# A two-layer encoder trunk: dense stages with a PSUM pool for each product bank, the last head's chunk in a tile of its own, and sums of squares on VectorE

## The chip, the cores and the metric

The kernel runs on one core of one Trainium2 chip. The metric is device time in microseconds for one execution; less is better. A core has engines that each work through a queue of their own in order: TensorE (PE in the profile; its weight loads are PEld), VectorE (DVE), ScalarE (ACT), GpSimd (POOL) and SyncE (SP), which issues DMA transfers. ScalarE issues some DMA transfers too. Matmul products land in PSUM, eight banks of 128 partitions by 512 f32 values; everything else lies in SBUF or in HBM.

## The reference

Two layers work on 1024 tokens of width 1024. In cut form:

```python
for i in range(2):
    h = rms_norm(x, norm_g[i])
    y = mixer_a(h, ...) if i == 0 else mixer_b(h, ...)   # attention, times silu(gate), @ w_out
    x = x + y
    g = sigmoid(rms_norm(x, ple_norm_g[i]) @ ple_w_gate[i])
    x = x + g * (p[i] @ ple_w_proj[i])
return rms_norm(x, final_norm_g)
```

`rms_norm(x, g)` is `x * rsqrt(mean(x*x) + 1e-6) * g`. Mixer A is 2-D neighbourhood attention of 16 heads with a bias table, mixer B grouped-query attention of 16 query and 4 key heads with normalised, rotated queries and keys. All is f32.

## The kernel before, in words

The program has four stages in a row: mixer A, dense stage 0, mixer B, dense stage 1. The mixers make the attention output times the gate, 128 channels (a pair of heads) at a time, and the dense stages do the rest of a layer: the output projection with the residual sum ("out"), and the gated input embedding ("ple").

**Numbers.** Each f32 operand of a projection is split into a high part, rounded to the matmul type f32r, and the low rest, and a product is three matmuls: high times high, high times low, low times high (`split3`, three calls of `mm`, L316). The activations stand transposed in two tiles, HTh and HTl, as [128 channels, 8 token tiles, 8 chunks of channels, 128 tokens]. `put` (L396 to L401) fills a chunk of four token tiles: ScalarE writes the high part (L400), VectorE the low one (L401). For the dense stages the chunks 0 to 6 of the mixer's output come back from HBM (`load_y`, L278, issued by ScalarE during the mixer's last head), and chunk 7, the last pair of heads, is written by `fin_last` (L471 to L480) straight from the mixer's end: VectorE multiplies (L472, L476; the second reads a PSUM bank "t" or "o" of the mixer for the second half of the tokens), ScalarE writes the high part (L479), VectorE the low one (L480).

**Weights** come in units of 128 x 1024 through two staging tiles (`Weights`, L184). `pump` is called once for each step of the program. It stages up to two units ahead (`stage`), but only `lag` (3) steps after the last split, and splits a unit no sooner than 3 steps after it was staged and when its pool has room: ScalarE copies the high part (L221), and VectorE makes the low part (L222) at the next step.

**A dense stage** (`dense_phase`, L1154) works in groups: "out" for token tiles 0 to 3, "out" for 4 to 7, then "ple" for the same; in dense stage 1 the last "ple" group is halved into tiles 4, 5 and tiles 6, 7. A group makes eight chunks of 128 output channels, each with the product over eight contraction steps, 24 matmuls, in two half-chunks (`parts`); the first group of a stage does the first halves of chunks 0 to 3 ahead of their second halves. Each chunk takes a PSUM bank from the pool `ps_d` (six banks, in turn); transposes use `ps_t` (two banks).

When a chunk's product is ready, `evac` reads it. For "out", VectorE adds it to the residual XR (L1224). For "ple", VectorE multiplies by the norm's factor (L1228), ScalarE applies tanh (L1229), and VectorE multiplies with the embedding and adds to XR (L1232, L1233). Then ScalarE squares the new chunk (L1216) and GpSimd adds the square to the group's sum `acc` (L1219); the first chunk's square starts the sum (L1213). These steps are put on short lists (`soon`, `rest`) that are worked off between half-chunks, one entry of `rest` at a step, so that each engine's queue is an order written out by hand. After a group come, as entries of `rest`, the eight `put`s for the next projection, the norm (`norm`: PE transposes `acc`, L1184, VectorE sums over tokens' rows, L1185, then L404 and GpSimd's power of -0.5, L405), and the spread of the factor over all partitions (`turn`: PE, L409, and a ScalarE copy, L1191). For the final groups the order is two empty entries, the norm, an empty one, the spread and the store (L1282, one multiplication for two chunks, the last on GpSimd).

The last group of all ends in `end` (L1248 to L1266): transposes of `acc` and of the last square, one reduction on VectorE (L1254), the factor, its spread, a ScalarE copy of the spread (L1261), and the multiplications with their stores (L1263 to L1266).

**Mixer B starts** with projections of keys and values: for each token tile, two items of 12 matmuls with 256 columns, whose products stand in turn in the one bank "d" and the bank "o", and are read by ScalarE (L996). What the last dense group left on `rest` is worked off between them.

**PSUM pools**, in the order of their banks: mixer A has "d" (0, 1), "s" (2, 3), "t" (4, 5), "o" (6, 7); a dense stage has `ps_d` (0 to 5) and `ps_t` (6, 7); mixer B has "d" (0), "s" (1 to 4), "t" (5, 6), "o" (7). A pool is opened where the stage before it closed its own. The framework puts in the waits that a tile needs before its memory is used again.

Of the kernel before, what the change touches and what calls it, by code (L numbers as in the profile page):

```python
# [11 lines left out]
F32 = mybir.dt.float32  # L12
F32R = mybir.dt.float32r
# [3 lines left out]
ALU = mybir.AluOpType  # L17
# [4 lines left out]
NT = 8  # L22
# [133 lines left out]
def trunk(ctx, tc, x, xT, wts, bias, gains, hgains, mask, rope, out):  # L156
# [13 lines left out]
    HTh = glob.tile([128, NT, KC, 128], F32R, name="HTh")  # L170
    HTl = glob.tile([128, NT, KC, 128], F32R, name="HTl")
# [106 lines left out]
    def load_y(l, t):  # L278
        for d, src in zip((HTh, HTl), yD[l]):
            act.dma_start(d[:, t, 0:7].bitcast(F32), src[t, :, 0:7])  # L280
# [73 lines left out]
    def proj_T(key, hf, alloc, evac, release=(), kstep=None):  # L354
# [3 lines left out]
        for k0, k1 in chunks(KC, kstep):  # L358
            def f(k0=k0, k1=k1):
# [3 lines left out]
                rh = HTh[:, 4 * hf:4 * hf + 4]  # L363
                rl = HTl[:, 4 * hf:4 * hf + 4]
                for k in range(k0, k1):
                    c = slice(k * 128, (k + 1) * 128)
                    split3(st["ps"], wh[:, c], wl[:, c], rh[:, :, k, :], rl[:, :, k, :], k == 0, k == KC - 1)
# [7 lines left out]
    def proj_N(keys, t, ncol, alloc, evac, release=(), kstep=None):  # L375
# [5 lines left out]
        for k0, k1 in chunks(nk, kstep):  # L381
            def f(k0=k0, k1=k1):
                if k0 == 0:
                    st["ps"] = alloc()
                for k in range(k0, k1):
                    wh, wl = WQ.get(keys[k // per])
                    c = slice((k % per) * ncol, (k % per + 1) * ncol)
                    split3(st["ps"], HTh[:, t, k, :], HTl[:, t, k, :], wh[:, c], wl[:, c], k == 0, k == nk - 1)
# [7 lines left out]
    def put(src, gi, hf, k, eng=None):  # L396
# [3 lines left out]
        act.activation(HTh[:, ts, k, :], src, AF.Copy, scale=g)  # L400
        dve.scalar_tensor_tensor(HTl[:, ts, k, :], src, g, HTh[:, ts, k, :], op0=ALU.mult, op1=ALU.subtract)  # L401
# [9 lines left out]
    def head_end(sb, h, hf, rs, Ops, ylive, layer, gg, talloc):  # L411
# [59 lines left out]
        def fin_last():  # L471
# [7 lines left out]
            act.activation(HTh[:, ts, 7, :], y3, AF.Copy)  # L479
            dve.tensor_tensor(HTl[:, ts, 7, :], y3, HTh[:, ts, 7, :], ALU.subtract)  # L480
# [53 lines left out]
    def mixer_a():  # L534
        with ExitStack() as es:
            one = es.enter_context(tc.tile_pool(name="aone", bufs=1))
            pd = es.enter_context(tc.tile_pool(name="apd", bufs=2, space=PSUM))
            psS = es.enter_context(tc.tile_pool(name="aps", bufs=2, space=PSUM))
# [29 lines left out]
            def v_first(hf, banks, k):  # L568
                wh, wl = WQ.get(("av", 0, k // 4))
                c = slice((k % 4) * 256, (k % 4 + 1) * 256)  # L570
                for i in range(3):
                    for t in range(4):
                        a = (HTh, HTh, HTl)[i][:, 4 * hf + t, k, :]
# [580 lines left out]
    def dense_phase(l):  # L1154
        with ExitStack() as es:
# [4 lines left out]
            ps_d = es.enter_context(tc.tile_pool(name="dps", bufs=6, space=PSUM))  # L1160
            ps_t = es.enter_context(tc.tile_pool(name="dpt", bufs=2, space=PSUM))
# [3 lines left out]
            WQ.cap[2] = WSLOTS  # L1165
            for c in range(4):
                WQ.get(("out", l, c))
# [3 lines left out]
            def alloc():  # L1171
                return ps_d.tile([128, 512], F32, name="d")
# [21 lines left out]
            def group(kind, ta, tb, final, to, gi):  # L1194
# [15 lines left out]
                def square(c):  # L1210
# [8 lines left out]
                    pool.tensor_tensor(acc, acc, sq, ALU.add)  # L1219
# [28 lines left out]
                def end(sq):  # L1248
                    ps = talloc()
# [132 lines left out]
```

## Time and profile before

| | us |
|---|---|
| three runs | 1554.23, 1554.27, 1555.39 (median 1554.27) |
| the profiled execution | 1555.67 |
| its span, first to last instruction | 1553.9 |
| PE busy | 1505.5 |
| VectorE busy | 996.4 |
| ScalarE busy | 857.6 |
| GpSimd busy | 401.7 |
| mean granted clock of TensorE | 0.991 |

Times in a row of a timeline are the start from the beginning of the span and the duration. In square brackets stands how long the engine had been idle before, and what ended the idle time as far as semaphores tell. "L316 PE MATMUL d<-HTh,wh" is a matmul issued on line 316 whose product goes to the tile "d" with HTh and wh as its operands; "x24" at a row's end are 24 merged instructions. Matmuls are pipelined, so the pace of a run of them is read from one start to the next and not from the duration. A busy share of PE over the whole span is an average over stages: what matters here is where PE has no work.

### The profile page before, as it was taken

Reading aid. Unit: us, or ns where it says so; the run is one execution under the profiler, and the core shown is the slowest. Engines: PE = TensorE matmul, PEld = TensorE weight load, DVE = VectorE, ACT = ScalarE, POOL = GpSimd, SP = SyncE. Lnnn points to the kernel's source line nnn. Section 1 sums busy time; section 2 is a strip of 40 time slices with the busy share of each in tenths; the row PEclk is TensorE's granted clock in tenths of the full one; section 3 lists DMA queues with packets and bytes.
Section 4 is the critical chain, followed back from the end, with each engine's and each line's share of the span. In section 5 each row is a group of like instructions: output and inputs, shape, how many; then the busy total and the mean of one; then the engine's idle time right before and its main releaser. Section 6 shows DMA issues by size and latency. Waiting matters only on the chain.

```text
span 1553.9 us, 24232 instructions
## 1 busy us (share of the span) xinstructions
PE 1505.5 (97%) x9058; PEld 1325.3 (85%) x9058; DVE 996.4 (64%) x1678; ACT 857.6 (55%) x1663; POOL 401.7 (26%) x507
## 2 busy tenths in 40 slices
PE   8999999999999899998999999999999999899997
PEld 8789889888988688888988889989888888778886
DVE  4675675576576334667867777677777887624475
ACT  7564554555456423335476666766667767513343
POOL 1231232223222032122512234445132200022133
PEclk9999999999999999999999999999999999999998
DMA  7221311221125942242200111111101214633122
GB/s 298 78 65 43 106 47 59 84 62 56 64 77 156 333 132 89 93 149 77 70 20 22 48 50 46 57 39 52 42 21 42 89 35 151 207 127 104 57 82 95
DMA packets 91621, 136.91 MB, mean 88 GB/s; under 512 B 13296, under 2 KB 54384, under 8 KB 91504
## 3 DMA queue, kind: packets, MB, share of 16 engines
q1 hardware_dynamic: 86496, 120.29, 23.8%
q10 hardware_dynamic: 5008, 15.08, 2.8%
q8 instruction: 71, 1.16, 0.3%
q14 instruction: 46, 0.38, 0.1%
HBM read 102.72 MB, written 32.62 MB: 87 GB/s over the span
## 4 chain that ended last, share of the span: by engine, by line
PE 74%; DVE 13%; ACT 8%; issue 3%; DMA 1%; ACTq 0%; POOL 0%; DVEq 0%; SPq 0%; POOLq 0%
PE d L316 47%; PE o L316 10%; PE s L316 8%; PE t L1074 5%; DVE PTl L1077 2%; PE t L663 2%; DVE mn L1058 2%; DVE wl L222 2%; DVE th L1232 1%; ACT PTh L1076 1%; DVE HTl L401 1%; DVE XR L1233 1%; ACT wh L221 1%; ACT HTh L400 1%; ACT P L1064 1%
## 5 line engine op out<-in xcount | busy, mean ns | idle before, releaser
L316 PE MATMUL d<-HTh,wh 128*128 128x512 f32 (+1 forms) x1080 | 419.0, 388 | 5.6 <-issue 4.7
L316 PE MATMUL d<-HTh,wl 128*128 128x512 f32 (+1 forms) x1080 | 409.7, 379 | 1.5 <-DVE wl L222 1.5
L316 PE MATMUL d<-HTl,wh 128*128 128x512 f32 (+1 forms) x1080 | 409.3, 379 | 0.0
L1077 DVE TENSOR_TENSOR PTl<-t,PTh 128x512 fp32r<-128x512 f32 x256 | 164.5, 684 | 123.8 <-ACT PTh L1076 123.0
L316 PEld LDWEIGHTS d<-HTh,wl 128*128 128x128 f32 x1080 | 203.9, 189 | 41.2 <-DVE wl L222 1.9
L316 PEld LDWEIGHTS d<-HTh,wh 128*128 128x128 f32 x1080 | 204.2, 189 | 37.1 <-issue 5.1
L316 PEld LDWEIGHTS d<-HTl,wh 128*128 128x128 f32 x1080 | 204.5, 189 | 30.2
L1064 ACT ACTIVATE P<-s,mn 128x1024 f32<-128x1024 f32 x128 | 142.6, 1114 | 58.6 <-DVE mn L1058 58.2
L1219 POOL TENSOR_TENSOR acc<-acc,sq 128x512 f32<-128x512 f32 (+1 forms) x62 | 75.6, 1219 | 368.5 <-ACT sq L1216 368.5
L1076 ACT ACTIVATE PTh<-t 128x512 fp32r<-128x512 f32 x256 | 139.5, 592 | 40.8 <-PE t L1074 40.1
L316 PE MATMUL d<-wh,HTh 128*128 128x256 f32 x544 | 153.9, 290 | 7.2 <-ACT sq L1216 4.3
L1058 DVE TENSOR_REDUCE mn<-s 128x1 f32<-128x1024 f32 x128 | 154.8, 1209 | 9.3 <-PE s L316 9.1
L316 PE MATMUL d<-wl,HTh 128*128 128x256 f32 x544 | 151.2, 285 | 0.0
L316 PE MATMUL d<-wh,HTl 128*128 128x256 f32 x544 | 151.1, 285 | 0.0
L1074 PE MATMUL t<-ident,P 128*128 128x128 f32 x1024 | 137.7, 275 | 8.2 <-DVE PTl L1077 5.9
L1074 PEld LDWEIGHTS t<-ident,P 128*128 128x128 f32 x1024 | 114.6, 141 | 24.5 <-DVE PTl L1077 18.5
L316 PE MATMUL s<-KA,QS 128*128 128x512 f32 (+2 forms) x384 | 133.7, 402 | 0.0
L316 PE MATMUL o<-PTh,V 128*128 128x256 f32 (+2 forms) x672 | 119.2, 288 | 3.2 <-ACT P L1064 1.1
L316 PE MATMUL s<-KB,QS 128*128 128x512 f32 (+2 forms) x384 | 121.6, 371 | 0.0
L222 DVE TENSOR_TENSOR wl<-wstage,wh 128x1024 fp32r<-128x1024 f32 x86 | 108.6, 1268 | 20.4 <-ACT wh L221 18.9
L316 PE MATMUL o<-PTl,V 128*128 128x256 f32 (+2 forms) x672 | 118.8, 288 | 0.3 <-DVE PTl L667 0.3
L1216 ACT ACTIVATE sq<-XR 128x512 f32<-128x512 f32 (+1 forms) x63 | 36.8, 585 | 142.9 <-DVE XR L1224 88.1
(178 smaller groups left out, 2623.4 us busy)
## 6 DMA issues: line engine op xcount, KB each, us to landing
wstage<-in_wts SPq DMA_DIRECT2D x92, 512.0 KB
rb<-rD SPq DMA_DIRECT2D x56, 128.0 KB
ppD<-th SPq DMA_DIRECT2D x24, 256.0 KB
pp<-ppD SPq DMA_DIRECT2D x24, 256.0 KB
XT<-in_xT SPq DMA_DIRECT2D x8, 512.0 KB
X<-in_x SPq DMA_DIRECT2D x8, 512.0 KB
XR<-in_xT SPq DMA_DIRECT2D x16, 256.0 KB
xD<-XR SPq DMA_DIRECT2D x16, 256.0 KB
```

Of the source, the lines that this page charges most:

```text
L221: act.activation(hi, s, AF.Copy)
L222: self.rest = lambda: dve.tensor_tensor(lo, s, hi, ALU.subtract)
L316: pe.matmul(ps, a, b, start=first, stop=last, skip_group_check=True)
L400: act.activation(HTh[:, ts, k, :], src, AF.Copy, scale=g)
L663: pe.transpose(ps[:, i], sp[:, i * 128:(i + 1) * 128], ident)
L1058: dve.tensor_reduce(mn, ps, axis=AX.X, op=ALU.min)
L1064: act.activation(p, ps, AF.Exp, bias=mn, scale=-1.0, accum_out=RS[h, hf][:, t:t + 1])
L1074: pe.transpose(ps[:, i], p[:, k * 128:(k + 1) * 128], ident)
L1076: act.activation(PTh[:, ks, c], ps, AF.Copy)
L1077: dve.tensor_tensor(PTl[:, ks, c], ps, PTh[:, ks, c], ALU.subtract)
L1216: act.activation(sq, xr, AF.Square)
L1219: pool.tensor_tensor(acc, acc, sq, ALU.add)
```

## The change

- The six banks of one pool `ps_d` become four pools of one bank each, taken in turn; the turn starts with bank 0 in dense stage 0 and with bank 1 in dense stage 1. `ps_t` gets four banks. In mixer A the pools "s" and "d" change places, so "s" has banks 0 and 1.
- Chunk 7 of HTh and of HTl goes into a tile of its own; `HTh(t, k)` and `HTl(t, k)` pick the tile.
- In the dense stages the weights' `lag` is 2 and not 3.
- The squares are added to `acc` by VectorE and not by GpSimd.
- In the final groups five empty entries instead of two stand ahead of the norm.
- At the end, matmuls with a column of 1/1024 make the mean of the squares in one product, in place of transposes and a reduction; the factor is spread into two banks, one for VectorE, one for ScalarE's copy; the stores are cut smaller and ordered otherwise.

The core of the diff:

```diff
+    mean1 = glob.tile([128, 1], F32, name="mean1")
+    pool.memset(mean1, 1.0 / D)
+    HT = {c: (glob.tile([128, NT, 7, 128], F32R, name=f"HT{c}"), glob.tile([128, NT, 128], F32R, name=f"H7{c}")) for c in "hl"}
+    def HTh(t, k):
+        return HT["h"][0][:, t, k] if k < 7 else HT["h"][1][:, t]
...
     def mixer_a():
+            psS = es.enter_context(tc.tile_pool(name="aps", bufs=2, space=PSUM))
             pd = es.enter_context(tc.tile_pool(name="apd", bufs=2, space=PSUM))
-            psS = es.enter_context(tc.tile_pool(name="aps", bufs=2, space=PSUM))
...
     def dense_phase(l):
-            ps_d = es.enter_context(tc.tile_pool(name="dps", bufs=6, space=PSUM))
-            ps_t = es.enter_context(tc.tile_pool(name="dpt", bufs=2, space=PSUM))
+            ps_d = [es.enter_context(tc.tile_pool(name=f"dps{i}", bufs=1, space=PSUM)) for i in range(4)]
+            ps_t = es.enter_context(tc.tile_pool(name="dpt", bufs=4, space=PSUM))
+            turn_d = [l]
+            WQ.lag = 2
             def alloc():
-                return ps_d.tile([128, 512], F32, name="d")
+                turn_d[0] += 1
+                return ps_d[(turn_d[0] - 1) % 4].tile([128, 512], F32, name="d")
...
-                    pool.tensor_tensor(acc, acc, sq, ALU.add)
+                    dve.tensor_tensor(acc, acc, sq, ALU.add)
...
                 def end(sq):
-                    ps = talloc()
+                    ps = talloc()[:, 0, :n]
                     for i in range(n):
-                        pe.transpose(ps[:, i], acc[:, i * 128:(i + 1) * 128], ident)
+                        mm(ps[:, i:i + 1], acc[:, i * 128:(i + 1) * 128], mean1, i == 0, False)
                     for i in range(n):
-                        pe.transpose(ps[:, n + i], sq[:, i * 128:(i + 1) * 128], ident)
-                    dve.reduce_sum(ms, ps.rearrange("p (s t) c -> p t s c", s=2), axis=AX.XY)
+                        mm(ps[:, i:i + 1], sq[:, i * 128:(i + 1) * 128], mean1, False, True)
-                    roots(ms, rt[:, ta:tb])
-                    ps = talloc()
+                    dve.tensor_scalar(ms, ps, EPS, None, op0=ALU.add)
+                    pool.tensor_tensor(rt[:, ta:tb], ms, neghalf[:, 0:n], ALU.pow)
+                    ps, ps2 = talloc(), talloc()
                     spread(ps, rt[:, ta:tb])
+                    spread(ps2, rt[:, ta:tb])
                     rr = ps[:, :n].rearrange("p t c -> p (t c)")
-                    act.activation(R[:, cols], rr, AF.Copy)
-                    for a, b, q in ((0, 3, sync), (3, 6, act)):
+                    act.activation(R[:, cols], ps2[:, :n].rearrange("p t c -> p (t c)"), AF.Copy)
+                    for a, b, q in ((0, 1, sync), (1, 2, act), (2, 4, sync), (4, 6, act)):
                         dve.tensor_tensor(X[:, a:b], X[:, a:b], rr[:, None].to_broadcast([128, b - a, w]), ALU.mult)
                         q.dma_start(out[a:b, :, cols].rearrange("c p t -> p c t"), X[:, a:b])
-                    pool.tensor_tensor(X[:, 6:8], X[:, 6:8], R[:, cols][:, None].to_broadcast([128, 2, w]), ALU.mult)
-                    sync.dma_start(out[6:8, :, cols].rearrange("c p t -> p c t"), X[:, 6:8])
+                        if a == 1:
+                            for c in (6, 7):
+                                pool.tensor_tensor(X[:, c], X[:, c], R[:, cols], ALU.mult)
+                                sync.dma_start(out[c, :, cols], X[:, c])
...
-                    rest.extend([lambda talloc: None, lambda talloc: None, norm, lambda talloc: None, turn, lambda talloc, f=store: f()])
+                    wait = lambda talloc: None
+                    rest.extend([wait] * 5 + [norm, wait, turn, lambda talloc, f=store: f()])
...
             WQ.cap[2] = 0
+            WQ.lag = LAG
```

27 lines of the change are left out of this document (13 added, 14 removed).

## The prediction

> **What bounds the kernel now.** I read the page's summary and chain first, then PE's timeline at the four places where a stage begins or ends, then the VectorE, ScalarE and GpSimd timelines beside them.
>
> ```profile
> span 1553.9 us, 24232 instructions
> ...
> PE 1505.5 (97%) x9058; PEld 1325.3 (85%) x9058; DVE 996.4 (64%) x1678; ACT 857.6 (55%) x1663; POOL 401.7 (26%) x507
> ...
> PE 74%; DVE 13%; ACT 8%; issue 3%; DMA 1%; ACTq 0%; POOL 0%; DVEq 0%; SPq 0%; POOLq 0%
> ```
>
> PE is busy nearly always and carries three quarters of the chain, and the change leaves its number of long matmuls as it is. So only two things can move the time: stretches in which PE stands still, and stretches in which its matmuls run slowly. PE's timeline shows five such places at or inside the dense stages. The first is the start of dense stage 0:
>
> ```profile
> 528.08 0.76 PE L316 MATMUL d<-HTh,wh 128*128 128x512 f32 x1 [4.66 <-issue]
> ...
> 528.64 0.63 PE L316 MATMUL d<-HTl,wh 128*128 128x512 f32 x1
> ...
> 533.76 0.49 PE L316 MATMUL d<-HTl,wh 128*128 128x512 f32 x1
> ```
> ```profile
> 525.89 0.69 DVE L480 TENSOR_TENSOR HTl<-Y,HTh 128x512 fp32r<-128x512 f32 x1 [0.83 <-ACT HTh L479]
> ...
> 527.29 0.69 DVE L476 TENSOR_TENSOR Y<-Y,t 128x512 f32<-128x512 f32 x1
> ...
> 529.28 2.35 DVE L222 TENSOR_TENSOR wl<-wstage,wh 128x1024 fp32r<-128x1024 f32 x2
> ```
>
> PE stands still for 4.66 us and goes on 0.10 us after 527.98, where L476 ends. L476 has nothing to do with the first matmul's data: it reads mixer A's transpose bank "t". The six product banks of the dense stage are one pool and lie over "d", "s" and "t" of mixer A, so I read this as a wait of the pool's first tile for all that lay under the pool. L480, which writes the last head's chunk of the first half, ends at 526.58, also after PE stopped. The start of mixer B has the same shape:
>
> ```profile
> 707.00 0.39 PE L316 MATMUL d<-HTh,wl 128*128 128x512 f32 x1
> ...
> 707.68 0.39 PE L316 MATMUL d<-HTh,wl 128*128 128x512 f32 x1
> ...
> 712.39 0.55 PE L316 MATMUL d<-wh,HTh 128*128 128x256 f32 x1 [4.32 <-ACT sq L1216]
> ...
> 712.74 0.41 PE L316 MATMUL d<-wl,HTh 128*128 128x256 f32 x1
> ...
> 718.07 0.38 PE L316 MATMUL o<-wh,HTl 128*128 128x256 f32 x1
> ...
> 719.72 0.28 PE L316 MATMUL o<-wh,HTh 128*128 128x256 f32 x1
> ...
> 720.68 0.28 PE L316 MATMUL o<-wh,HTl 128*128 128x256 f32 x1
> ...
> 727.35 0.36 PE L316 MATMUL d<-wh,HTh 128*128 128x256 f32 x1
> ```
> ```profile
> 711.56 0.68 DVE L1228 TENSOR_TENSOR th<-d,RG 128x512 f32<-128x512 f32 x1
> ```
>
> The releaser named is a square on ScalarE, whose result these matmuls don't read. What ends at 712.24, 0.15 us before, is the evacuation (L1228) of the last dense chunk, which by the order of allocation sits in bank 1, while mixer B's first tile is bank 0. Again the pool was waited for, not the bank.
>
> Both stalls are followed by slow matmuls. Full pace is 0.227 us for 512 columns (707.00 to 707.68 is three steps) and 0.12 us for 256 (719.72 to 720.68, eight steps). After 528.64 twelve steps take 5.12 us, 0.427 each; after 712.74 twenty-five take 5.33 us, 0.213 each. Half pace costs 12 x 0.200 + 0.3 in the step from 528.08 = 2.7 us at the first place and 25 x 0.093 = 2.3 us at the second.
>
> **Part by part.** *A, start of dense stage 0.* With one pool to a bank, the first two chunks lie over mixer A's "s", done long before, the next two over "d", and with the last head's chunk apart the first four contraction steps don't touch what L480 writes. So PE can start at 523.42, when its last matmul ends, and the stall and the slow pace go: 4.66 + 2.7 = 7.4 us. What is late next is the low part of chunk 2's weights: chunks 0 and 1 take 24 x 0.227 = 5.45 us, the third matmul of chunk 2 would come at 529.32, and the first of the two L222 ends at 529.28 + 1.18 = 530.46. That gives 1.1 us back: 6.2 us. Bounds: 1.5 (PE waits for L480 after all and still slows) to 7.4.
>
> *B, start of mixer B.* PE can start at 708.07 instead of 712.39. Tiles t0 and t1 take 2 x 24 x 0.12 = 5.8 us, to 713.8. Then t2 needs the bank of t0, so ScalarE's evacuation (L996):
>
> ```profile
> 715.16 0.63 ACT L1216 ACTIVATE sq<-XR 128x512 f32<-128x512 f32 x1 [2.25 <-DVE XR L1233]
> ...
> 717.93 0.47 ACT L996 ACTIVATE th<-d,rt 128x256 f32<-128x256 f32 x1 [0.92 <-POOL acc L1219]
> ```
> ```profile
> 715.93 1.29 POOL L1219 TENSOR_TENSOR acc<-acc,sq 128x512 f32<-128x512 f32 x1 [2.14 <-ACT sq L1216]
> ```
> ```profile
> 670.49 0.68 DVE L1228 TENSOR_TENSOR th<-d,RG 128x512 f32<-128x512 f32 x1
> ...
> 688.75 0.69 DVE L1232 SCALAR_TENSOR_TENSOR th<-th,pp 128x512 f32<-128x512 f32 x1
> ...
> 691.54 1.32 DVE L401 SCALAR_TENSOR_TENSOR HTl<-XR,GN,HTh 128x512 fp32r<-128x512 f32 x1 [1.37 <-ACT HTh L400]
> ...
> 694.78 0.75 DVE L401 SCALAR_TENSOR_TENSOR HTl<-XR,GN,HTh 128x512 fp32r<-128x512 f32 x1 [1.31 <-ACT HTh L400]
> ...
> 705.43 0.68 DVE L1228 TENSOR_TENSOR th<-d,RG 128x512 f32<-128x512 f32 x1
> ...
> 709.53 1.38 DVE L1232 SCALAR_TENSOR_TENSOR th<-th,pp 128x512 f32<-128x512 f32 x1 [0.70 <-ACT th L1229]
> ```
>
> L996 is the end of a VectorE-ScalarE chain that runs behind PE: five chunks from 670.49 to 705.43 take 6.99 us each, PE's 24 x 0.227 = 5.45. The adds on VectorE change it thus. A VectorE instruction beside a GpSimd add is drawn out (L1232 1.38 for 0.69, L401 1.32 for 0.75); with GpSimd idle that goes. An add of 0.69 us (an SBUF-to-SBUF step as wide as L1232) comes in, and VectorE waits for the square ahead of it, 0.63 us. In chunks that also write a next-stage chunk (L401), the add falls into the 1.37 us in which VectorE waits for ScalarE anyway, so they shorten by some 0.55 us: five of them, 2.7 us. In the last two, which have no L401, 0.63 + 0.69 + 0.1 comes in and 0.7 goes: +0.7 each, 1.4 us. The final add ends 0.6 us sooner than GpSimd's. L996 moves from 717.93 to about 716.0, t2 starts at 716.5, and t4 after two tiles and two sets of four transposes (5.8 + 0.8) at 723.1 instead of 727.35. ScalarE's eight next-stage chunks, which t4 needs too, are taken to fit in that time; the lower bound covers it if they don't. B is 4.3 us; bounds 2.3 (the chain gets no shorter: t2 at 718.4, t4 at 725.0) and 6.6 (stall and slow pace both go whole).
>
> *C, D: two shorter stalls in dense stage 1.*
>
> ```profile
> 1355.77 0.50 PE L316 MATMUL d<-HTh,wh 128*128 128x512 f32 x1 [0.74 <-ACT th L525]
> ...
> 1396.07 0.50 PE L316 MATMUL d<-HTh,wl 128*128 128x512 f32 x1 [1.47 <-DVE wl L222]
> ```
>
> C: the first chunk there takes bank 1, which lies over "s", so the 0.74 us until the last "d" is evacuated goes (0 to 0.74). D: the weights of chunk 7 are split one step before their use, so the low part comes late. With a lag of 2, counted through the pump's rule (stage two, age three steps), the splits move from steps 6, 7, 13 to 5, 6, 11; chunk 7 is used in step 14. D gives 1.5 us (0 to 1.5).
>
> *E, the first sum of squares in the last group.*
>
> ```profile
> 1498.08 0.66 PE L1184 MATMUL t<-ident,acc 128*128 128x128 f32 x4 [3.39 <-POOL acc L1219]
> ```
>
> The transposes of the sum stand in PE's queue after three half-chunks; PE waits 3.39 us for GpSimd's last add. Three places later are 3 x 12 x 0.12 = 4.3 us more: E is 3.4 us, if the chain does not carry its delay on to the end. In the narrow groups a chunk of PE is 24 x 0.12 = 2.9 us, and the chain is this:
>
> ```profile
> 1541.53 0.42 DVE L1228 TENSOR_TENSOR th<-d,RG 128x256 f32<-128x256 f32 x1 [1.08 <-PE d L316]
> ...
> 1542.44 0.43 DVE L1232 SCALAR_TENSOR_TENSOR th<-th,pp 128x256 f32<-128x256 f32 x1 [0.48 <-ACT th L1229]
> ...
> 1542.90 0.42 DVE L1233 TENSOR_TENSOR XR<-th,XR 128x256 f32<-128x256 f32 x1
> ```
> ```profile
> 1543.42 0.42 ACT L1216 ACTIVATE sq<-XR 128x256 f32<-128x256 f32 x1 [0.61 <-DVE XR L1233]
> ```
>
> From 1541.53 to the square's end at 1543.84 are 2.3 us; with an add of 0.42 and 0.1 to hand over it is 2.8, just under 2.9, and the store multiplications, which come three steps later too, are on top. So the bounds are 0 and 3.4.
>
> *F, the end.*
>
> ```profile
> 1544.43 0.69 DVE L1254 TENSOR_REDUCE ms<-t 128x2 f32<-128x512 f32 x1 [1.11 <-PE t L1253]
> ...
> 1546.89 0.38 ACT L1261 ACTIVATE R<-t 128x256 f32<-128x256 f32 x1 [2.52 <-PE t L409]
> ...
> 1547.31 1.82 DVE L1263 TENSOR_TENSOR XR<-XR,t 128x768 f32<-128x768 f32 x2 [1.98 <-ACT R L1261]
> ```
>
> The reduction goes (0.69), and the multiplications no longer wait for ScalarE's copy (0.42). The matmul with a column of 1/D replaces transposes; no such f32 matmul is in the trace. Its bounds are a transpose pair and several times that, 0 to +1.5; I take +0.5, nearest to the pair. A smaller first piece starts the store earlier, and two more store issues follow: about even. F is 0.7, from -1 to +1.5.
>
> The other edits cost nothing on the path: one 128x1 memset before the first load has landed, and four product banks for six. the L1228 at 705.43, of chunk 5, ends 9 us behind PE's last matmul of that chunk (707.91 less two chunks of 5.45 is 697.0), and four banks leave three chunks, 16.4 us.
>
> Sum: 6.2 + 4.3 + 0.7 + 1.5 + 3.4 + 0.7 = 16.8 us. The profiled execution took 1555.67 us (span 1553.9 and 1.8 around it), so 1538.9 in its terms. The median of the three runs, 1554.27, lies 1.4 lower: 1537.5.
>
> **Rivals.** *R1, the waits stay.* The first matmuls wait for something else at nearly the same time (L480 at 526.58, or a pool lying under a new one). For it: L480 ends late. Against: 0.10 us behind L476 and 0.15 behind L1228. A, B and C go: 16.8 - 11.2 = 5.6 us gain, 1548.7.
>
> *R2, slower: VectorE becomes the bound.* If the adds cost their full trip (0.63 + 0.69 + 0.1 = 1.4 us a chunk) and no contention is given back, a chunk takes 8.4 us of chain against PE's 5.45. Over eight chunks VectorE falls 23.6 us behind, four banks cover 16.4, PE waits 7.2 us in each of three wide groups of this kind: 21.6 us, more than the 16.8 gained, 1559. It decides from 5.45 + 16.4 / 8 = 7.5 us a chunk. Against: the 1.37 us waits ahead of L401. [...]
>
> *R3, the slow pace stays at mixer B.* A wait of 2.7 us is left there (713.8 to 716.5), after which PE could go at half pace again: +2.3 us, 1539.8. The trace has slow matmuls behind 4.66 and 4.32 us and none behind 3.39. [...]
>
> *R4, D and E are not realised.* The splits stay late, or the chain carries its delay into the tail: 16.8 - 4.9 = 11.9, 1542.4.
>
> **How the numbers follow.** Forecast 0.50, R4 0.20, R1 0.12, R3 0.08, R2 0.05, no effect that can be seen 0.05. About 0.2%, 3.1 us, is what a measurement of this kernel can tell from no change. Faster: 0.50 + 0.20 + 0.12 + 0.08, and a little more for partial R1, 0.91; same 0.04; slower 0.05. The forecast's own range is 1533.5 to 1541, with A and B at their upper bounds at one end and E half lost at the other. Taking in R3 and R4 and part of R1's side it is 1533 to 1547, leaving out R1's centre, R2 and no effect, about 0.2.
>
> **What would show it.** Right: PE's first dense matmul within 0.2 us of its last mixer one at both starts, no 0.427 us steps there, a wait near 1 us at chunk 2, mixer B's first tile right behind the last dense matmul and a wait of 2 to 3.5 us before t2; no wait at chunk 7 or before L1184's successor; L1232 at 0.69 everywhere but beside the stores. Wrong: a wait of over 3 us at either start, evacuations over 10 us behind PE, or PE waiting in the middle of a wide group for a bank.

## The result, and the profile after

The changed kernel takes 1539.62 us (median of four runs, 1538.12 to 1541.13), the kernel before 1554.66 beside it (1554.23 to 1555.39): a ratio of 0.9903, 95% interval 0.9886 to 0.992, so 15.0 us less. The profiled execution took 1540.83 us, with a span of 1539.0.

The page of the changed kernel, its summary and its chain:

```profile
span 1539.0 us, 24188 instructions
...
PE 1501.8 (98%) x9064; PEld 1323.4 (86%) x9064; DVE 1014.8 (66%) x1741; ACT 859.3 (56%) x1663; POOL 327.2 (21%) x447
...
PE 78%; DVE 10%; ACT 5%; issue 5%; DMA 1%; POOL 1%; ACTq 0%; POOLq 0%; SPq 0%; DVEq 0%
```

VectorE took over GpSimd's adds (62 of them), yet PE's share of the chain rose. Line numbers are now those of the changed kernel: `mm` is L324, the weights' low part L230, the last head's low write L487, the add of a square L1229, the evacuation L1238, the gate L1242, the sum's transposes L1194, the spread L416, mixer B's evacuation L1003.

The start of dense stage 0, PE's and VectorE's timelines:

```profile
524.94 0.40 PE L324 MATMUL d<-wh,wl 128*128 128x512 f32 x1
525.17 0.39 PE L324 MATMUL d<-HTh,wh 128*128 128x512 f32 x1
...
530.86 0.39 PE L324 MATMUL d<-HTl,wh 128*128 128x512 f32 x1
532.58 0.50 PE L324 MATMUL d<-HTh,wl 128*128 128x512 f32 x1 [1.33 <-DVE wl L230]
```
```profile
530.70 0.69 DVE L487 TENSOR_TENSOR H7l<-Y,H7h 128x512 fp32r<-128x512 f32 x1 [0.70 <-ACT H7h L486]
531.31 2.35 DVE L230 TENSOR_TENSOR wl<-wstage,wh 128x1024 fp32r<-128x1024 f32 x2
```

The first product stands 0.23 us, one ordinary step, behind mixer A's last matmul, where 4.66 us were idle. The wait that is left is for chunk 2's low weights, behind the last head's low write on VectorE. No step of 0.427 us follows.

The start of mixer B, on PE, VectorE and ScalarE:

```profile
703.62 0.39 PE L324 MATMUL d<-H7h,wl 128*128 128x512 f32 x1
703.85 0.28 PE L324 MATMUL d<-wh,HTh 128*128 128x256 f32 x1
...
711.42 0.66 PE L1194 MATMUL t<-ident,acc 128*128 128x128 f32 x4 [1.66 <-DVE acc L1229]
712.28 0.38 PE L324 MATMUL d<-wh,HTh 128*128 128x256 f32 x1 [0.20 <-ACT th L1003]
...
719.23 0.65 PE L416 MATMUL t<-ident,rt 128*128 128x128 f32 x4 [0.95 <-POOL rt L412]
```
```profile
707.12 0.68 DVE L1238 TENSOR_TENSOR th<-d,RG 128x512 f32<-128x512 f32 x1
...
710.67 0.69 DVE L1229 TENSOR_TENSOR acc<-acc,sq 128x512 f32<-128x512 f32 x1 [0.76 <-ACT sq L1226]
```
```profile
711.77 0.45 ACT L1003 ACTIVATE th<-d,rt 128x256 f32<-128x256 f32 x1
```

Mixer B's first tile follows the dense stage's last matmul at once. It starts 3.27 us before the evacuation of the last dense chunk does (L1238 at 707.12), whose end the kernel before had to wait for. Between the second tile and the third PE waits 1.66 us for VectorE's last add of a square, and 0.20 us more for the first tile's evacuation (L1003).

In dense stage 1, chunk 7's third matmul and VectorE's split that it needs, then the sums and the spread among the last two groups:

```profile
1386.05 0.39 PE L324 MATMUL d<-HTl,wh 128*128 128x512 f32 x1
1386.27 0.39 PE L324 MATMUL d<-HTh,wl 128*128 128x512 f32 x1
...
1488.87 0.60 PE L1194 MATMUL t<-ident,acc 128*128 128x128 f32 x4
...
1492.18 0.60 PE L416 MATMUL t<-ident,rt 128*128 128x128 f32 x4
```
```profile
1381.19 1.22 DVE L230 TENSOR_TENSOR wl<-wstage,wh 128x1024 fp32r<-128x1024 f32 x1
```

None of these PE rows has a bracket: nothing is waited for. The low weights are ready 3.9 us ahead (1381.19 + 1.22 to 1386.27). The tail on PE, and its first multiplications on VectorE:

```profile
1527.77 0.58 PE L324 MATMUL t<-mean,acc 128*128 128x1 f32 x4
1530.07 0.82 PE L324 MATMUL t<-mean,sq 128*128 128x1 f32 x4 [1.72 <-ACT sq L1226]
1531.99 1.12 PE L416 MATMUL t<-ident,rt 128*128 128x128 f32 x4 [1.10 <-POOL rt L1267]
```
```profile
1532.71 1.95 DVE L1274 TENSOR_TENSOR XR<-XR,t 128x256 f32<-128x256 f32 x4 [1.56 <-PE t L416]
```

From the square's matmuls to the spread are 1.92 us. In the kernel before they were 2.28, from the square's transposes to the spread:

```profile
1543.89 0.44 PE L1253 MATMUL t<-ident,sq 128*128 128x128 f32 x2 [1.56 <-ACT sq L1216]
1546.17 0.69 PE L409 MATMUL t<-ident,rt 128*128 128x128 f32 x2 [1.84 <-POOL rt L405]
```

**A ledger of places.** All these kernels issue the same matmuls of `mm` in the same order up to the last chunk's end; only the transposes for sums and spreads change places among them. So the start of the n-th of these matmuls in one trace less its start in another tells by how much the one is late there, and the change of that number across a place is what the place costs. Kernel before less changed kernel: program start and mixer A -1.91 us, start of dense stage 0 +5.98, start of mixer B +3.65, the rest of mixer B -0.55, first product of dense stage 1 +1.01, its chunk 7 +1.80, its last two groups +3.78, the end +1.08. The sum is 14.83, the two spans' difference. The negative entries are in places whose order of work the change leaves as it is.

### The profile page after: what moved, and what is told of

It reads as the page before. It is cut to its first block, busy times and chain, and to the rows that moved or that the text cites. A ratio compares the mean times of both kernels' runs of the same rounds, so it can differ in the third digit from the quotient of the medians.

```text
span 1539.0 us, 24188 instructions
## 1 busy us (share of the span) xinstructions
PE 1501.8 (98%) x9064; PEld 1323.4 (86%) x9064; DVE 1014.8 (66%) x1741; ACT 859.3 (56%) x1663; POOL 327.2 (21%) x447
## 4 chain that ended last, share of the span: by engine, by line
PE 78%; DVE 10%; ACT 5%; issue 5%; DMA 1%; POOL 1%; ACTq 0%; POOLq 0%; SPq 0%; DVEq 0%
PE d L324 52%; PE o L324 9%; PE s L324 8%; PE t L1081 5%; DVE PTl L1084 2%; PE t L670 2%; DVE mn L1065 2%; ACT PTh L1083 1%; DVE wl L230 1%; ACT P L1071 1%; ACT wh L229 1%; PE t L1035 1%; DMA ppD<-G 0%; DVE Y L430 0%; DVE G L509 0%
## 5 line engine op out<-in xcount | busy, mean ns | idle before, releaser
L324 PE MATMUL d<-HTh,wh 128*128 128x512 f32 (+1 forms) x945 | 366.6, 388 | 0.0
L324 PE MATMUL d<-HTh,wl 128*128 128x512 f32 (+1 forms) x945 | 357.6, 378 | 1.3 <-DVE wl L230 1.3
L324 PE MATMUL d<-HTl,wh 128*128 128x512 f32 (+1 forms) x945 | 357.3, 378 | 0.0
L324 PEld LDWEIGHTS d<-HTh,wl 128*128 128x128 f32 x945 | 177.8, 188 | 36.1 <-DVE wl L230 1.8
L324 PEld LDWEIGHTS d<-HTh,wh 128*128 128x128 f32 x945 | 178.1, 188 | 25.6 <-DVE G L509 0.4
L324 PEld LDWEIGHTS d<-HTl,wh 128*128 128x128 f32 x945 | 178.4, 189 | 25.1
L324 PE MATMUL d<-wh,HTh 128*128 128x256 f32 x476 | 134.4, 290 | 3.4 <-ACT wh L241 3.1
L324 PE MATMUL s<-KA,QS 128*128 128x512 f32 (+2 forms) x384 | 133.6, 402 | 0.0
L324 PE MATMUL d<-wl,HTh 128*128 128x256 f32 x476 | 131.8, 284 | 0.0
L324 PE MATMUL d<-wh,HTl 128*128 128x256 f32 x476 | 131.7, 284 | 0.0
L324 PE MATMUL o<-PTh,V 128*128 128x256 f32 (+2 forms) x672 | 119.2, 288 | 3.7 <-ACT PTh L673 1.2
L324 PE MATMUL s<-KB,QS 128*128 128x512 f32 (+2 forms) x384 | 121.6, 370 | 0.0
L230 DVE TENSOR_TENSOR wl<-wstage,wh 128x1024 fp32r<-128x1024 f32 x86 | 108.5, 1268 | 18.7 <-ACT wh L229 17.4
L324 PE MATMUL o<-PTl,V 128*128 128x256 f32 (+2 forms) x672 | 118.9, 288 | 0.3 <-DVE PTl L674 0.3
L229 ACT ACTIVATE wh<-wstage 128x1024 fp32r<-128x1024 f32 x86 | 89.6, 1051 | 41.3 <-PE d L324 27.2
L674 DVE TENSOR_TENSOR PTl<-t,PTh 128x384 fp32r<-128x384 f32 (+1 forms) x128 | 66.8, 522 | 63.8 <-ACT PTh L673 62.7
```

Source lines behind the costliest of these rows:

```text
L229: act.activation(hi, s, AF.Copy)
L230: self.rest = lambda: dve.tensor_tensor(lo, s, hi, ALU.subtract)
L324: pe.matmul(ps, a, b, start=first, stop=last, skip_group_check=True)
L674: dve.tensor_tensor(PTl[:, sl], ps[:, :m], PTh[:, sl], ALU.subtract)
```

## The experiments

Each kernel is the changed one with one thing altered, except where said. Kernels 1 to 4 shared a chip, 5 to 8 another, 9 to 12 a third. The kernel before ran beside them and took 1557.3, 1557.54 and 1557.92 us, some 3 us more than on the chip of the result. Number 12 is the changed kernel itself; on the other two chips it was not run, and number 2, whose ledger is nearly that of the changed kernel, stands for it on the first. Medians of four runs (five for number 7), with the ratio to the kernel before and its interval, and five entries of the ledger (each kernel less the first trace of the changed one, us):

| kernel | us | ratio | dense 0 start | mixer B start | dense 1 start, chunk 7 | last two groups | end |
|---|---|---|---|---|---|---|---|
| before, first trace | - | - | 5.98 | 3.65 | 2.81 | 3.78 | 1.08 |
| 1 old PSUM | 1549.15 | 0.9949 [0.9931, 0.9967] | 4.85 | 3.12 | 1.04 | 0.00 | 0.32 |
| 2 one tile | 1538.89 | 0.9884 [0.9867, 0.99] | -0.16 | -0.01 | 0.00 | 0.00 | -0.12 |
| 3 adds on GpSimd | 1540.13 | 0.9891 [0.9877, 0.9906] | 0.23 | -0.17 | -0.01 | 0.93 | 0.42 |
| 4 lag 3 | 1546.06 | 0.9929 [0.9914, 0.9944] | -0.11 | 2.60 | 1.75 | 2.00 | 0.11 |
| 5 early norm | 1541.33 | 0.9899 [0.9885, 0.9914] | -0.15 | 0.35 | -0.01 | 0.94 | 0.15 |
| 6 old end | 1540.15 | 0.9891 [0.9874, 0.9908] | -0.15 | 0.01 | 0.03 | -0.01 | 1.25 |
| 7 PSUM, tile only | 1550.63 | 0.9962 [0.9949, 0.9975] | -0.12 | 1.53 | 1.77 | 6.94 | 1.41 |
| 8 two moves | 1547.08 | 0.9935 [0.992, 0.995] | 0.13 | 5.75 | 0.00 | -0.03 | -0.46 |
| 9 old order | 1539.75 | 0.9884 [0.9866, 0.9903] | -0.15 | 0.01 | -0.01 | -0.02 | -0.20 |
| 10 one pool of 4 | 1543.34 | 0.9907 [0.9891, 0.9924] | -0.14 | 1.91 | 1.01 | 0.00 | -0.25 |
| 11 norm one later | 1537.14 | 0.9872 [0.9852, 0.9892] | -0.11 | -0.72 | 0.00 | 0.00 | -0.37 |
| 12 changed again | 1539.65 | 0.9887 [0.9866, 0.9908] | -0.11 | 0.35 | 0.00 | 0.00 | -0.10 |

Number 12 shows what the ledger can tell: 0.4 us at a place. Its 0.35 has a cause of its own, told in the last section. Places that are not in the table vary more: against its own first trace the changed kernel lost 1.7 us at the end of mixer A in number 12 and gained 1.0 at the program's start.

**1. The old PSUM layout.**

```diff
-            psS = es.enter_context(tc.tile_pool(name="aps", bufs=2, space=PSUM))
             pd = es.enter_context(tc.tile_pool(name="apd", bufs=2, space=PSUM))
+            psS = es.enter_context(tc.tile_pool(name="aps", bufs=2, space=PSUM))
...
-            ps_d = [es.enter_context(tc.tile_pool(name=f"dps{i}", bufs=1, space=PSUM)) for i in range(4)]
-            ps_t = es.enter_context(tc.tile_pool(name="dpt", bufs=4, space=PSUM))
+            ps_d = es.enter_context(tc.tile_pool(name="dps", bufs=6, space=PSUM))
+            ps_t = es.enter_context(tc.tile_pool(name="dpt", bufs=2, space=PSUM))
...
-                return ps_d[(turn_d[0] - 1) % 4].tile([128, 512], F32, name="d")
+                return ps_d.tile([128, 512], F32, name="d")
```

> The changed kernel with the PSUM of before: one pool of six product banks and two small tiles in the dense stages, and mixer A's PSUM pools in the old order; chunk 7's own tile, lag 2, the adds on VectorE, the late norm and the new end stay. Theory (the forecast's terms A, B and C hang on the banks): TensorE's stops of about 4.4 us at the start of dense stage 0 and of about 4.5 us at the start of mixer B come back, and the 0.7 us at dense stage 1; 11 us worked out from the forecast's 6.2 + 4.3 + 0.7, so about 1550.5 us, between 1547 and 1553. Rival (chunk 7's own tile and the adds did it, the pools nothing): the time of the changed kernel, 1539.6 us within 1 us, and TensorE's first product of dense stage 0 right behind mixer A's last matmul.

Measured 1549.15 us. PE and VectorE at the start of dense stage 0:

```profile
528.03 0.39 PE L324 MATMUL d<-wh,wl 128*128 128x512 f32 x1
533.07 0.47 PE L324 MATMUL d<-HTh,wh 128*128 128x512 f32 x1 [4.65 <-issue]
...
534.41 0.63 PE L324 MATMUL d<-HTl,wh 128*128 128x512 f32 x1
534.83 0.63 PE L324 MATMUL d<-HTh,wl 128*128 128x512 f32 x1
```
```profile
532.28 0.69 DVE L483 TENSOR_TENSOR Y<-Y,t 128x512 f32<-128x512 f32 x1
```

The stop is back to a hundredth (4.65), it ends 0.10 us behind the read of mixer A's "t", and the half pace follows (0.42 a step). Mixer B and the first product of dense stage 1 lose their parts too. The theory holds: A, B and C hang on the layout of the pools, 9.0 us by the ledger where 11 were worked out.

**2. One tile for all chunks.**

```diff
-    HT = {c: (glob.tile([128, NT, 7, 128], F32R, name=f"HT{c}"), glob.tile([128, NT, 128], F32R, name=f"H7{c}")) for c in "hl"}
+    HT = {c: glob.tile([128, NT, KC, 128], F32R, name=f"HT{c}") for c in "hl"}
```

> The changed kernel with all eight chunks of the normalised activation in one tile again, for the high and for the low part; everything else stays. Theory (the pools alone free TensorE at the start of dense stage 0 only if its operand is free too): the first product now waits for the last head's low write by VectorE, so 3 to 5 us of the stop come back there and nowhere else, 1542.5 to 1545 us. Rival (the pools alone did it, or the tracked wait is by region and not by tile): the time of the changed kernel, 1539.6 within 1 us, with no stop before the first product of dense stage 0.

Measured 1538.89 us, and no entry of the ledger above 0.2. The theory fell. PE and VectorE:

```profile
524.68 0.39 PE L324 MATMUL d<-HTh,wh 128*128 128x512 f32 x1
```
```profile
527.32 0.69 DVE L487 TENSOR_TENSOR HTl<-Y,HTh 128x512 fp32r<-128x512 f32 x1 [0.90 <-ACT HTh L486]
```

PE reads chunk 0 of the tile 2.64 us before VectorE begins to write chunk 7 of the same tile. Only the part that is read is waited for, so chunk 7's own tile is worth nothing here.

**9. The old order of mixer A's pools, the new dense pools.** The first half of experiment 1's diff alone.

> The changed kernel with mixer A's PSUM pools in the old order (d, then s); the four single product pools of the dense stages stay, and now the first two lie over mixer A's d. Theory (a tile of a pool waits for all that lay under its pool, and under a single bank that is one bank): the first product of dense stage 0 waits only for the last d of mixer A to be evacuated, about 1 us after TensorE's last matmul there; 0.5 to 1.5 us lost, without slow matmuls after it, and nothing at mixer B or in dense stage 1. Rival (the order carries term A): TensorE waits for L483, some 4 to 6 us lost there.

Measured 1539.75 us. PE at the start:

```profile
524.06 0.40 PE L324 MATMUL d<-wh,wl 128*128 128x512 f32 x1
525.48 0.50 PE L324 MATMUL d<-HTh,wh 128*128 128x512 f32 x1 [1.02 <-ACT G L532]
```

PE does wait for the last "d" to be evacuated, and the theory's 1 us is there. But the wait at chunk 2 is gone, since PE comes there later: the place costs nothing (-0.15), so neither the theory's loss nor the rival's came.

**10. The four product banks as one pool.**

```diff
-            ps_d = [es.enter_context(tc.tile_pool(name=f"dps{i}", bufs=1, space=PSUM)) for i in range(4)]
+            ps_d = es.enter_context(tc.tile_pool(name="dps", bufs=4, space=PSUM))
...
-            turn_d = [l]
...
-                turn_d[0] += 1
-                return ps_d[(turn_d[0] - 1) % 4].tile([128, 512], F32, name="d")
+                return ps_d.tile([128, 512], F32, name="d")
```

> The changed kernel with the four product banks of the dense stages as one pool of four, not four pools of one; the order of mixer A's pools and all else stay. Theory (a pool is waited for as a whole): at dense stage 0 the pool lies over s and d but no longer over t, so at most 1.5 us are lost; at mixer B and dense stage 1 the pool is again released by its last evacuation, so 3 to 4 us are lost at mixer B and up to 1 us at dense stage 1; 4 to 6 us in all. Rival (four banks instead of six and the order are what matters, the single pools nothing): less than 1 us lost in the ledger of stages.

Measured 1543.34 us, 3.7 more than number 12. PE and VectorE at mixer B, then PE at dense stage 1's first product:

```profile
704.53 0.39 PE L324 MATMUL d<-H7h,wl 128*128 128x512 f32 x1
708.86 0.55 PE L324 MATMUL d<-wh,HTh 128*128 128x256 f32 x1 [3.94 <-DVE th L1236]
...
1350.48 0.50 PE L324 MATMUL d<-HTh,wh 128*128 128x512 f32 x1 [0.74 <-ACT th L532]
```
```profile
708.03 0.68 DVE L1236 TENSOR_TENSOR th<-d,RG 128x512 f32<-128x512 f32 x1
```

Mixer B waits for the pool's last evacuation (L1236 here, 0.15 us before), which by the order of allocation sits in bank 3, while mixer B's first tile is bank 0: it is the pool that is waited for. The place loses 1.91 us, less than the 3 to 4 expected; the half granted clock behind the wait lasts 3.4 us, where number 1 has 6.8. The start of dense stage 0 loses nothing (-0.14): four banks reach over "s" and "d" but not over "t", and that is enough for A. Dense stage 1's first product waits 0.74 us for mixer B's last "d" (L532), as in the kernel before. Without the turn its first chunk lies in bank 0, on that "d" itself, so for C this doesn't tell the single pools from the choice of the bank.

**4. Lag 3.**

```diff
-            WQ.lag = 2
+            WQ.lag = 3
```

> The changed kernel with weights split three units ahead of the due place in the dense stages, as before, instead of two. Theory (term D, the late split of chunk 7's weights): the wait of 1.5 us before chunk 7 in dense stage 1 comes back, and with the adds on VectorE perhaps 3 us before the last narrow group's spread, so 1541 to 1544.6 us. Rival (D was hidden by something else and lag does nothing): 1539.6 within 0.7 us.

Measured 1546.06 us, 7.2 more than number 2 on the same chip. PE at mixer B, at chunk 7 and in the last groups:

```profile
712.38 0.66 PE L1194 MATMUL t<-ident,acc 128*128 128x128 f32 x4 [3.93 <-DVE acc L1229]
...
1388.60 0.50 PE L324 MATMUL d<-HTh,wl 128*128 128x512 f32 x1 [1.46 <-DVE wl L230]
...
1496.59 0.65 PE L416 MATMUL t<-ident,rt 128*128 128x128 f32 x4 [1.78 <-POOL rt L412]
```

The last two are the theory's. The first was in neither expectation, and it takes the time 1.5 us over the theory's bound. VectorE's last split ahead of it, with lag 3 and then with lag 2:

```profile
698.61 1.22 DVE L230 TENSOR_TENSOR wl<-wstage,wh 128x1024 fp32r<-128x1024 f32 x1
```
```profile
693.48 1.22 DVE L230 TENSOR_TENSOR wl<-wstage,wh 128x1024 fp32r<-128x1024 f32 x1
```

With lag 3 one more split falls among the last dense chunks, where VectorE is behind. PE stood 1.31 us earlier in this trace, and the last add ends 0.96 later (712.32 for 711.36), so it is 2.3 us later against PE.

**3. The adds on GpSimd.**

```diff
-                    dve.tensor_tensor(acc, acc, sq, ALU.add)
+                    pool.tensor_tensor(acc, acc, sq, ALU.add)
```

> The changed kernel with the adds of the squares on GpSimd as before. Theory (the adds are beside the path on either engine; what they cost is taken up by the slack behind TensorE): within 0.6 us below to 2 us above the changed kernel, 1539 to 1541.6 us, with VectorE's evacuating operations longer where an add of GpSimd's runs beside them (some 1.4 us for 0.69). Rival (moving the adds to VectorE was what freed the path in the wide groups): 3 to 6 us are lost, 1542.6 to 1545.6 us. Opposite rival (VectorE became the tighter engine by the adds): 2 us or more are won, under 1537.6 us.

Measured 1540.13 us, 1.2 more than number 2; the ranges of the two overlap. The two kernels' rows for the gate step, grouped by line, changed kernel first (durations least/median/most, ns):

```profile
L1242 DVE SCALAR_TENSOR_TENSOR th<-th,pp x40: 410/685/694, 623.2 to 1528.7; 128x512 f32<-128x512 f32 x24, 128x256 f32<-128x256 f32 x16
```
```profile
L1242 DVE SCALAR_TENSOR_TENSOR th<-th,pp x40: 410/686/1424, 621.9 to 1526.4; 128x512 f32<-128x512 f32 x24, 128x256 f32<-128x256 f32 x16
```

The drawn-out gates (up to 1424 ns) are there only with the adds on GpSimd, and each of them overlaps an instruction of GpSimd. By the ledger the adds on GpSimd cost 0.93 us before the spread of the last groups and 0.42 at the end. In the wide groups, and at the start of mixer B (-0.17), they cost nothing that it can tell.

**5 and 6. The early norm; the old end.** Number 5 has the first line's change; in number 6 all of `end` is that of the kernel before, of which the rest of the diff shows the core.

```diff
-                    rest.extend([wait] * 5 + [norm, wait, turn, lambda talloc, f=store: f()])
+                    rest.extend([wait] * 2 + [norm, wait, turn, lambda talloc, f=store: f()])
...
-                        mm(ps[:, i:i + 1], sq[:, i * 128:(i + 1) * 128], mean1, False, True)
+                        pe.transpose(ps[:, n + i], sq[:, i * 128:(i + 1) * 128], ident)
+                    dve.reduce_sum(ms, ps.rearrange("p (s t) c -> p t s c", s=2), axis=AX.XY)
...
-            for a, b, q in ((0, 1, sync), (1, 2, act), (2, 4, sync), (4, 6, act)):
+            for a, b, q in ((0, 3, sync), (3, 6, act)):
```

> The changed kernel with the norm of dense stage 1's narrow groups three places earlier, as before. Theory (term E): TensorE again reaches the sums and the spread before VectorE and GpSimd have delivered, and loses up to 3.4 us: 1540.2 to 1543 us. Rival (since the adds left GpSimd the norm's input comes early enough at the old place): 1539.6 within 0.6 us.

> The changed kernel with the old ending of the last group (transposes and one long sum on VectorE, two stores less). Theory (term F, 0.7 forecast, about 1.1 in the two traces): 1540 to 1541.5 us. Rival (the fp32 matmuls with one column cost what the transposes and the sum cost): 1539.6 within 0.4 us.

Measured 1541.33 and 1540.15 us. The early norm costs 0.94 and the old end 1.25 by the ledger, the first within its theory's bounds, the second within its own.

**7. PSUM and tile alone.** The diffs of 3, 4, 5 and 6 together: adds on GpSimd, lag 3, the early norm, the old end.

> Only the PSUM pools and chunk 7's own tile of the change; adds on GpSimd, three units ahead, the early norm and the old ending as before. Theory (A, B and C hang on these two alone, 10 to 11 us, and the other parts give the remaining 4 to 6): 1543.7 to 1545.2 us. Rival (the parts depend on each other, so that the freed time comes back as other waits in the dense stages): 1547 us or more.

Measured 1550.63 us. The rival holds. PE in the last groups:

```profile
1490.88 1.11 PE L1194 MATMUL t<-ident,acc 128*128 128x128 f32 x4 [3.88 <-POOL acc L1229]
```

The place costs 6.94 us: 3.88 of wait, and some 3.1 in a half granted clock behind it (1490.04 to 1496.87). The lag, the adds and the norm undone one at a time cost 2.00, 0.93 and 0.94 there, 3.87 together, at different waits and none of them with half clock; that the wait here is as long as their sum may be chance. So what comes on top of the single prices is the half clock. The kernel before lost 3.78 at this place: it waited 3.39 us, and its clock stayed full. At mixer B lag 3 costs 1.53 here, with the adds on GpSimd, and 2.60 in number 4, with the adds on VectorE.

**8 and 11. The waits that are left at mixer B.** Number 8, then number 11:

```diff
+            WQ.settle()
             post.flush()
...
-                    rest.insert(5, norm)
+                    rest.insert(8 if kind == "ple" and tb == NT else 5, norm)
```
```diff
-                    rest.insert(5, norm)
-                    rest.append(turn)
+                    last = kind == "ple" and tb == NT
+                    rest.insert(6 if last else 5, norm)
+                    rest.extend([lambda talloc: None] * last + [turn])
```

> The changed kernel with two moves at the stage starts: the planned weight units are settled at the end of mixer A ahead of the last head's closing operations on VectorE, so that chunk 2's low weights come first, and the norm of dense stage 0's last group is put three places later into mixer B. Theory (what was left of the starts, 1.5 us of wait for chunk 2's low weights and 1.7 + 1.0 us for the accumulated squares and the root in mixer B): both go, 1536.6 us, between 1535.5 and 1538.5. Rival (VectorE is the one that is late, so moving its work only moves the wait to chunk 7 or to mixer B's third tile): 1539.6 within 1 us, with waits of the same size further on.

> The changed kernel with the norm of dense stage 0's last group one place later in mixer B (between its first two tiles instead of ahead of them) and the spread of its root one place later than that. Theory (what is left at mixer B's start is TensorE reaching the sums and the spread too early, 1.66 and 0.95 us): both waits go, 2 to 2.6 us less between the last matmul of dense stage 0 and the fifth tile of mixer B. Rival (VectorE and ScalarE are the late ones, so the wait moves): a wait of the same size before the spread or before the fifth tile, no gain; or a loss of some us as with the norm three places later.

> The changed kernel once more, beside the others on the same chip. Both theories: within 1.5 us of 1539.6 where the kernel before is within 1.5 us of 1554.7, and in proportion to it (0.990) where it isn't. The stages are expected as in its first trace; a different time would come from a half granted clock at the start of the program or at the end of mixer A.

Measured 1547.08, 1537.14 and 1539.65 us. PE in number 8, then in number 11:

```profile
714.34 0.39 PE L324 MATMUL d<-wh,HTh 128*128 128x256 f32 x1 [2.51 <-ACT th L1004]
...
724.94 1.12 PE L416 MATMUL t<-ident,rt 128*128 128x128 f32 x4 [4.16 <-POOL rt L412]
```
```profile
710.66 0.39 PE L324 MATMUL d<-wh,HTh 128*128 128x256 f32 x1 [2.52 <-ACT th L1003]
...
718.39 0.60 PE L416 MATMUL t<-ident,rt 128*128 128x128 f32 x4
```

Number 8 lies outside both of its expectations. In both kernels the wait for the sum became a wait for the first tile's evacuation, the one that the prediction foresaw for the third tile. Number 8 put the sum right ahead of its own spread, so the whole chain of reduction and root lay open, 4.16 us, with half clock behind it. Its settling gained nothing at dense stage 0: the wait at chunk 2 went, and waits of 0.72 and 0.52 us for other weights came behind it. Number 11 left three entries between them. Its gain at mixer B is 0.72 us by the ledger; the 2.5 us by which its median is lower than number 12's are more than that, and the intervals of the two overlap. Whether it beats the changed kernel is not settled. Number 12 took as long as in the result, though the kernel before took 3.3 us more on this chip; in proportion it should have taken 1542.3. So the gain is 18.3 us here and 15.0 there, with intervals of the two ratios that overlap; what makes the difference was not found.

## Why the prediction was right, step by step

It gave 1537.5 us and 16.8 us of gain; measured were 1539.62 and 15.0. The mechanism was right in the main, with B's second part and E's cause excepted, and the terms of the sum came out so:

| term | forecast | ledger |
|---|---|---|
| A, start of dense stage 0 | 6.2 | 5.98 |
| B, start of mixer B | 4.3 | 3.65 |
| C, first product of dense stage 1 | 0.7 | 1.01 |
| D, chunk 7's weights | 1.5 | 1.80 |
| E, the late norm | 3.4 | 3.78 |
| F, the end | 0.7 | 1.08 |
| sum | 16.8 | 17.3 |
| places not touched | 0 | -2.47 |

- **The reading of the two stalls** (a pool is waited for as a whole) was right: experiments 1 and 10. Two details were not needed. "The last head's chunk apart" gives nothing (experiment 2), and the first chunks lying over "s" give nothing net (experiment 9). Keeping the products off "t" is enough for A (experiment 10); six single pools were not run. For C the pool and the choice of the bank were not told apart.
- **A.** The wait left at chunk 2 was forecast at 1.1 us and is 1.5 (530.86 + 0.23 to 532.58). The half pace went, as said.
- **B.** Seen from the last dense matmul, mixer B's first evacuation moved from 10.25 us (717.93 - 707.68) to 8.15 (711.77 - 703.62), 2.1 us; the forecast said 1.9. The gap between the second and third tile is 2.7, as forecast, 1.86 of it idle. But the 1.9 agrees by luck. The forecast took it from the adds, and with the adds on GpSimd the first evacuation stands 7.96 us behind the last dense matmul, no later (experiment 3). Nor did the wide chunks give it: the last chunk's evacuation ends at 707.80, 4.18 us behind the last dense matmul's start, where it was 4.56 (712.24 - 707.68), so 0.38 of the 2.1 lies ahead of it and the rest behind. The missing 0.65 us is the spread's wait for GpSimd's root (0.95 before 719.23), which the forecast had not in its path. And with the adds on VectorE some 2.3 of the 3.65 us need the lag of 2 (experiment 4's 2.60, less 0.35 for the half clock that its trace has there too, by number 12's price), which the forecast had put down under D alone; with the adds on GpSimd it is 1.53 (experiment 7).
- **The adds.** The contention went as forecast: L1242 never over 694 ns, where L1232 had 1423. The forecast's place for it was wrong: it counted on the wide groups, and experiment 3 finds the whole price, 1.35 us, in the last groups and the end. The rival R2, VectorE as the bound, fell: in the last group of dense stage 0 the evacuations come 6.0 us apart on average (665.00 to 707.12 over seven steps, 8.2 at most and 4.17 in the last three), under the 7.5 us at which R2 decides, and PE has no wait in it.
- **D** was right in kind and 0.3 short. **E** was right in size, but the late norm isn't shown to be its only cause: beside the lag of 2 and the adds on VectorE it is worth 0.94 (experiment 5), and with the norm late either of those undone costs 2.00 or 0.93 in the same groups (4, 3). The late norm with the old lag and the old adds was not run. **F** was 0.4 short; its working, 0.69 + 0.42 - 0.5, adds up to 0.6, and experiment 6 gives 1.25.
- **R3**, half pace at mixer B, came about in two traces, numbers 12 and 5, which are alike up to there, and cost 0.35 us in each, not 2.3: what the slow stretch loses, the wait before the spread gives back.
- **What the forecast lacked** is an entry for the places that it doesn't touch. The changed kernel's profiled execution lost 1.42 us in the first 20 us of the program against that of the kernel before: its granted clock was half for 6.83 us there (7.97 to 14.79), the other's for 3.41 (8.32 to 11.73). It lost 0.49 at the end of mixer A, where PE waited 1.22 us for ScalarE and 0.70 in the kernel before, and 0.55 in mixer B, whose cause is open. Without these it would have taken 1538.4, where the forecast in the same terms was 1538.9.

## What to carry to other kernels

When an engine stops at the border of two stages, look at what was reported just before it goes on, even if that has no data in common with it: here a PSUM pool was released as a whole, and splitting it, or keeping it off the banks that finish last, gave some 9 us by the ledger. Undo parts one at a time and all together before giving each its price, and look at the clock: the norm, the lag and the adds cost 0.9 to 2.0 us singly and 6.9 together, but 3.1 of that was a half granted clock behind the longer wait (3.88 us). A place where one wait is removed has the next one queued behind it; read its size from the trace (2.7 us at the third tile here) before moving work to fill it.

## What the runs showed of the hardware beyond that

**Half clock behind short waits.** PE waits at the end of mixer A for ScalarE (L673), from 0.53 us (number 3) to 2.31 (number 10) in kernels that are the same up to there. In the windows of number 12 (length, busy times of PE, PEld, DVE, ACT and POOL, then the granted clock) the clock is then halved for 3.4 us, and once more at the start of mixer B:

```profile
518.25:521.66 3.41, 1.73 (x9) 1.24 (x8) 1.62 (x4) 1.47 (x3) 0.00 (x0) 1.00 1.03 412
521.70:525.10 3.40, 3.40 (x11) 2.72 (x10) 1.10 (x2) 1.79 (x3) 0.00 (x0) 0.50 1.04 416
712.80:716.20 3.40, 3.36 (x15) 3.37 (x16) 2.60 (x5) 2.80 (x7) 0.00 (x0) 0.50 0.13 39
```

The waits before it, in number 7 (halved) and in the changed kernel's first trace (not halved):

```profile
519.49 0.44 PE L324 MATMUL o<-PTh,V 128*128 128x384 f32 x1 [1.21 <-ACT PTh L673]
```
```profile
520.67 0.44 PE L324 MATMUL o<-PTh,V 128*128 128x384 f32 x1 [1.22 <-ACT PTh L673]
```

At this place the matmuls kept their full pace behind waits of 0.53, 0.68, 1.01, 1.02 and 1.04 us (numbers 3, 11, 9, 2 and 4) and of 1.22 (the changed kernel's first trace). They went at half pace, 0.427 us a step of 512 columns for 0.23, behind waits of 1.21, 1.35, 1.40, 1.54, 1.71 and 2.31 us (numbers 7, 12, 6, 5, 1 and 10). At mixer B, where a step of 256 columns is 0.12 us at full pace and 0.213 at half, the full pace stayed behind waits of 1.65 us (number 2), 1.66 (the first trace and 6), 1.67 (9), 1.85 (3), 2.51 (8), 2.52 (11) and 3.54 (7). Half pace came behind 1.67 us (5), 1.68 (12), 3.93 (1 and 4), 3.94 (10) and 4.32 (the kernel before).

So the length of one wait doesn't tell the cases apart. Nor does PE's work in two stretches around a wait: in the first one of number 12 above PE is busy for 1.73 of 3.41 us, and half clock follows. In the kernel before, in its last groups, PE waits 3.39 us and the clock stays full, though a stretch there has less work, 1.57 us:

```profile
1493.12:1496.53 3.41, 1.57 (x14) 1.36 (x12) 2.45 (x3) 1.75 (x5) 1.30 (x1) 1.00 0.15 41
```

What sets the cases apart was not shown.

**Spread between runs.** Number 12 took 1538.00, 1538.41, 1540.90 and 1543.09 us at mean granted clocks of 0.998, 0.997, 0.994 and 0.993. Part of a difference of 2 us between two kernels of this family can thus be the clock. What sets the length of ScalarE's wait from run to run was not tried.
